# Four more Strassen steps, gate corners in another tile, a later product and quartered first weights in a hybrid pooling and convolution block (one core)

## Chip, cores and metric

The kernel runs on one core of a Trainium2 chip. The metric is the device time of one execution in microseconds (us); of the kernel before, three runs gave a median of 2419.91 us.

## What is computed

One decoder block on 256 tokens of width 4096, in float32: a norm, one large projection, two mixers, a gated merge, a projection back with a residual, and a norm.

```python
h = rmsnorm(x, norm_w)
u_p, z_p, u_c, b_c, c_c, z_c, g_logit = split(h @ w_in)        # 4096 -> 6 x 2048 and 2 x 4096
y_pool = pool(u_p, pool_w, pool_scale) * silu(z_p)             # trailing means over 2, 4, 8, 16 tokens, less the token; a 512 x 512 map per group
y_conv = b_c * conv3(c_c * u_c, conv_w, conv_b) * silu(z_c)    # causal, depthwise, three taps
br = stack(y_pool, y_conv) @ w_branch                          # two of 2048 -> 4096
merged = sum over the two of sigmoid(g_logit + gate_b) * br
out = rmsnorm(x + merged @ w_out, final_norm_w)
```

## The kernel before, in words

**Units and steps.** All large products have one form: 256 tokens by K channels times K by 1024 columns. A *unit* is one such product for 1024 output columns. The order of the units is: for each half of the conv channels cz, cb, cu, cc (z, b, u and c of the reference), for each half of the pool channels pz and pu, then eight gate units g0_0, g1_0, g0_1 ... g1_3, eight branch units b0_0, b1_0 ... b1_3, and four output units o0 to o3. A *step* of a unit takes 256 channels of K: 16 steps in a unit, 8 in a branch unit. Its weights, 256 x 1024 floats (1 MB), come in one DMA into one of three buffers of the tile `raw`.

**Float32 in two halves.** Each operand is split into a rounded high half (an ACT copy, `highs`, L54) and a low half, the rest (a VectorE subtraction, `lows`, L57); a product is three matmuls, high x high, high x low and low x high. The halves of the weights stand in the tile `ring`, which has 15 cells of 512 columns; a cell is free again after the last matmul that reads it. The halves of the other operand (x for the first units, then the branch outputs y, then the merged m) stand in `arena`, `extra` and `last_pair`; PE loads them as stationary.

**Plain and Strassen steps.** A plain step (P) has 8 blocks of 3 matmuls. A Strassen step (S) takes the 2 x 2 blocks of its operands and needs 7 products, 21 matmuls, in Winograd's form; for that VectorE makes four sums of weight blocks (tile `parts`, 4 instructions) and takes the low halves of 3 blocks and 4 sums: `added` and `split` in `Step.rest`. An S step uses 7 ring cells, a P step 4. Which steps are S is written out by hand in strings, one character a step: FIRST, SIX4, SEVEN3, EIGHT, HOST, SIX5, OUT3, B0, B1 (L34 to L43). HOST has 19 characters: besides the 16 steps it holds B, the pooling's band product (`band_sums`, L568), and two M, its 512 x 512 maps (`mix`, L594), of the pooling unit before. It is used by pz1, which holds pu0's, and by g0_0, which holds pu1's. After the second M four groups of transposes of Y follow in ticks, and fill E.

**Banks and corners.** The sums of a unit stand in eight PSUM banks. Four (`sums`) are copied by ACT to E or Y at the unit's end (`evacuate`). If it has S steps, the other four (`shared`), the corners, are copied by ACT to a place called the join's slot, summed by VectorE there (`corner_sums`: two adds and a subtraction), and added to the unit's result (`combine`). For most units the slot is the next of the three raw buffers, so that it stands in the rotation of the weight loads as one load would (`loaded`, `issue_load`). For branch units (`rotates` False) it is `last_pair`.

**Order of work.** Every engine keeps the order in which the program was written. `pump` (L897) issues, after each block of matmuls, whatever may go: the next weight load when the step three loads back is prepared, and the next piece of preparation (highs, sums, lows) of the steps up to four ahead, if ring cells are free. After each 6 matmuls a `tick` takes one entry of a queue of small works; each unit puts its epilogue there (`epi`), in which `gap(n)` leaves n ticks free. So the small works, the roundings of later weights and the copies out of PSUM stand on ACT and VectorE in one fixed order. Ticks also run *fills* (`Fill`): an operand of the branch or output units is brought from DRAM by a DMA of the POOL queue into `sa` or `sb`, and split into halves in a freed part of `arena` by ACT or VectorE. The POOL queue also carries the gate's bias, which is added in memory by an accumulating DMA (`gather`, 512 KB each), and the moves of gates and products.

**Branch units.** b0_c's epilogue, which runs within b1_c, multiplies by the gate: `mul(Y, E, Y)`, the *product*, one tick after the unit's end. b1_c's epilogue loads the second gate, multiplies, adds Y, and transposes the sum.

**The start.** Steps 0 to 15 of the first unit, cz0, also bring x: `fetch_x` loads a block into Y, and ACT and VectorE make the operand of it, directly for a P operand, or with sums (`x_sums`) for an S operand, though cz0 itself has P steps only. Its first step's weights come in four DMAs and are rounded by quarters; the other steps are rounded by one instruction per tile. The third step uses an operand with sums.

Of the kernel before, what the change touches and what calls it, by code (L numbers as in the profile page):

```python
# [17 lines left out]
D = 4096  # L18
# [16 lines left out]
FIRST = (0, 1, 8, 2, 9, 3, 10, 11, 4, 12, 13, 5, 14, 6, 15, 7)  # L35
OPENED = 12
SIX4 = "PPPPSPSPSPSPSPSP"
SEVEN3 = "PPPSPSPSPSPSPSPS"
EIGHT = "PSPSPSPSPSPSPSPS"
HOST = "PPPBPPMMPPSPSSPSSPS"  # L40
OUT3 = "PSPSPSPSPSPSSPPP"
B0 = "PPPPPSPS"
B1 = "PSPSPSPP"  # L43


# [1 line left out]
def hybrid_block(ctx: ExitStack, tc: tile.TileContext, x, xc, prm, rows_in, w_in, pool_w, w_branch, w_out, out):  # L47
# [174 lines left out]
    class Step:  # L222
# [7 lines left out]
        def first(self):  # L230
            if self.kind == "B":
                return []

            def rounded(cells):
                self.q = self.raw.rearrange("p (i c) -> p i c", i=4)
                self.cells = cells
                if self is steps[0]:
                    for i in range(4):
                        highs(cells[i:i + 1], self.q[:, i:i + 1])
                else:  # L240
                    highs(cells, self.q[:, 0:len(cells)])

            return [(3 if self.kind == "S" else 4, None, rounded)]

        def rest(self):
            if self.kind == "P":
                def rests(_):
                    if self is steps[0]:
                        for i in range(4):
                            lows(self.cells[i:i + 1], self.q[:, i:i + 1])  # L250
                    else:
                        lows(self.cells, self.q)

                return [(None, None, rests)] + self.mid
            if self.kind == "S":
                def added(_):
                    q = self.q
                    add(sums[:, 0:2], q[:, 3:4].to_broadcast([P, 2, NH]), q[:, 1:3])
                    add(sums[:, 2], sums[:, 0], q[:, 2])
                    add(sums[:, 3], sums[:, 2], q[:, 0])  # L260
                    lows(self.cells, q[:, 0:3])

                def split(cells):
                    self.sum_cells = cells
                    highs(cells[0:2], sums[:, 0:2])
                    highs(cells[2:4], sums[:, 2:4])
                    lows(cells, sums)

                return [(None, None, added)] + self.mid + [(4, None, split)]
            if self.kind == "B":  # L270
                def parts(cells):
                    self.cells = cells
                    highs(cells, quarters(E))
                    lows(cells, quarters(E))

                return [(4, lambda: self.unit.flags.get("base"), parts)]

            def pooled(cells):
                self.pool_cells = cells
                q = quarters(E)[:, 2 * self.g:2 * self.g + 2]  # L280
                highs(cells, q)
                lows(cells, q)

            return [(None, None, lambda _: lows(self.cells, self.q)),
                    (2, lambda: self.unit.flags.get(f"pooled{self.g}"), pooled)]
# [188 lines left out]
    def in_unit(name, col, epi, text, **kw):  # L474
        units.append(Unit(name, lambda i: w_in[col // NU, i], seq_x(text), x_ops, epi, scaled=True, **kw))
        units[-1].text = text
        return units[-1]
# [4 lines left out]
    def conv_units(c, first):  # L482
        base = 2 * HALF + c * NU

        def b_epi(u):
            def copy(j):
                act(chan(Y)[:, 2 * j:2 * j + 2], bankview(j))
            return gap(6) + transposes(E, copy) + [lambda: move(g_d[c], Y)]

        def c_epi(u):  # L490
            def copy(j):
                if j == 3:
                    for i in range(4):
                        act(chan(E)[:, 2 * i:2 * i + 2], bankview(i))

            def taps(j):
                v, y = chan(E)[:, 2 * j:2 * j + 2], chan(Y)
                for i in range(2):
                    b = 2 * j + i
                    kb = 8 * c + b  # L500
                    act(y[:, b], v[:, i], AF.Identity, scale=tap_col(2, kb), bias=bias_col(kb))
                for i in range(2):
                    b = 2 * j + i
                    kb = 8 * c + b
                    for s in (1, 2):
                        stt(y[:, b, s:], v[:, i, 0:T - s], tap_col(2 - s, kb), y[:, b, s:], ALU.mult, ALU.add)

            items = gap(6) + pairs(transposes(E, copy)) + gap(1)
            for j, n in enumerate((1, 5, 7, 7)):
                items += gap(n) + [lambda j=j: taps(j)]  # L510
            return items + [lambda: move(E, g_d[c])] + gap(6) + [lambda: mul(Y, Y, E), lambda: put(y_d[1, c], chan(Y))]

        in_unit(f"cz{c}", base + 3 * HALF, lambda u: silu_y(), FIRST if first else SIX4, dst=Y)
        in_unit(f"cb{c}", base + HALF, b_epi, EIGHT).urgent = lambda: mul(E, E, Y)
        in_unit(f"cu{c}", base, lambda u: gap(2) + band_items(0) if c == 0 else [], SEVEN3, dst=Y)
        in_unit(f"cc{c}", base + 2 * HALF, c_epi, EIGHT).urgent = lambda: mul(E, E, Y)

    def pool_units(c):
# [98 lines left out]
    def gate_unit(n, c):  # L617
        def epi(u):
            def bias(t):
                gather(E[:, t], gate_b[n, None, c * NU:(c + 1) * NU].to_broadcast([P, NU]))  # L620

            return gap(1) + [lambda: bias(0), lambda: bias(1)] + gap(12) + [
                lambda: act(E[:, 0], E[:, 0], AF.Sigmoid), None,
                lambda: act(E[:, 1], E[:, 1], AF.Sigmoid), lambda: move(gates_d[n, c], E)] + (
                    [lambda: move(Y, gates_d[0, 0])] if (n, c) == (1, 3) else [])
        text = HOST if (n, c) == (0, 0) else SIX4 if (n, c) == (1, 3) else EIGHT
        in_unit(f"g{n}_{c}", 6 * HALF + n * D + c * NU, epi, text)

    def spare():
        return last_pair["tile"].rearrange("p (a n) -> p a n", a=2)  # L630
# [1 line left out]
    def branch_unit(n, c):  # L632
        def epi(u):
            if n == 0:
                return gap(1) + [lambda: mul(Y, E, Y)]
            turned = spare() if c < 3 else Y

            def gated():
# [245 lines left out]
    def issue_load(s):  # L884
        i = s.load_index
        r = raw[:, i % NRAW]
        if isinstance(s, Join):
            s.slot = r.rearrange("p (i c) -> p i c", i=4)
            return
        if i == 0:  # L890
            for k in range(4):
                load(r[:, k * NH:(k + 1) * NH], s.src[:, k * NH:(k + 1) * NH])
        else:
            load(r, s.src)
        if i + 1 < 16:
            fetch_x(i + 1)
        s.raw = r  # L897
# [60 lines left out]
            state["limit"] = state["now"] + u.lead  # L958
        pump()

    fetch_x(0)
    pump()

    def room(o):
# [36 lines left out]
    for u in units:  # L1001
# [1 line left out]
            last_pair["stack"].close()  # L1003
            open_last(F32)
        if not u.rotates:
            u.join.slot = last_pair["tile"].rearrange("p (i c) -> p i c", i=4)
        if u is last_x:
            bands_open.close()
            more = ctx.enter_context(tc.tile_pool(name="more", bufs=1))
# [121 lines left out]
```

## Time and profile before

| | |
|---|---|
| median of 3 runs | 2419.91 us (2418.51 to 2421.69) |
| the profiled execution | 2420.03 us |
| its span, first to last instruction | 2418.3 us |
| matmuls on PE | 10515 |
| ACT busy | 1421.8 us (59%) |
| bytes moved | 547.07 MB, 226 GB/s |
| mean granted clock of PE | 0.994 |

The span is what the trace covers; 1.7 us of the time lie around it. PE is TensorE's matmuls, PEld its weight loads, DVE is VectorE, ACT ScalarE, POOL and SP the two that issue DMAs. L57 and L54 are helpers that issue nearly all VectorE and ACT work, so the tiles of a row say what it is: `ring<-raw` on ACT is a rounding of weights, on VectorE a low half; `parts` are Strassen sums, `raw<-raw` and `last_pair<-last_pair` on VectorE are corner sums, `E<-sums` on ACT is a copy out of PSUM. A row of the timeline tells start, duration, engine, line, operation, tiles, shape and count, and in brackets how long the engine was idle before it and what ended that.

### The profile page before, as it was taken

How to read it: one execution, taken by the hardware profiler on the slowest of the kernel's cores; microseconds unless marked ns; L12 is line 12 of the kernel's file. 1: busy time of each engine (PE TensorE's matmuls, PEld its weight loads, DVE VectorE, ACT ScalarE, POOL GpSimd, SP SyncE). 2: the span in 40 equal slices, each digit the busy share in tenths (PEclk: the TensorE clock that was granted, in tenths of full speed). 3: DMA queues.
4: the chain of work that ended last, by engine and by line, in shares of the span. 5: the costliest groups of instructions: out<-in, count | busy, mean ns of one | idle time of the engine just before them, and what ended most of it. 6: DMA issues, size and time to landing. Idle time of an engine off the chain costs nothing. (4 is left out here: it accounts for less than half of the span.)

```text
span 2418.3 us, 26848 instructions
## 1 busy us (share of the span) xinstructions
PE 2379.8 (98%) x10515; PEld 1960.6 (81%) x10515; DVE 2137.6 (88%) x1769; ACT 1421.8 (59%) x1367; POOL 85.6 (4%) x147
## 2 busy tenths in 40 slices
PE   8999999999999999999999999999899999999998
PEld 6888888888888888888888888888778887888886
DVE  8789989988989969969998999889788889899998
ACT  6655555655556556556666566665565555556664
POOL 0000000000000000000000000001100000000000
PEclk9999999999999999999999999999999999999999
DMA  8656546655646655655776576667666765758767
GB/s 331 225 193 226 191 175 244 234 199 204 220 177 231 228 192 192 225 191 187 266 244 204 215 261 242 209 224 272 229 245 212 264 233 208 257 192 273 246 217 267
DMA packets 82959, 547.07 MB, mean 226 GB/s; under 512 B 9488, under 2 KB 9488, under 8 KB 21776
## 3 DMA queue, kind: packets, MB, share of 16 engines
q1 hardware_dynamic: 69392, 485.52, 55.1%
q0 software_dynamic: 13008, 58.73, 8.0%
q8 instruction: 82, 1.34, 0.2%
q10 hardware_dynamic: 432, 1.11, 0.1%
q14 instruction: 45, 0.37, 0.0%
HBM read 519.10 MB, written 26.21 MB: 225 GB/s over the span
## 5 line engine op out<-in xcount | busy, mean ns | idle before, releaser
L937 PE MATMUL sums<-ring,arena 128*128 128x512 f32 x7515 | 1756.9, 391 | 20.5 <-DVE ring L57 9.4
L937 PEld LDWEIGHTS sums<-ring,arena 128*128 128x128 f32 x7515 | 1412.2, 188 | 319.7 <-DVE ring L57 12.3
L57 DVE TENSOR_TENSOR ring<-raw,ring 128x2048 fp32r<-128x2048 f32 (+3 forms) x526 | 938.6, 1796 | 167.0 <-ACT ring L54 163.5
L54 ACT ACTIVATE ring<-raw 128x2048 fp32r<-128x2048 f32 (+3 forms) x526 | 791.4, 1520 | 493.9 <-PE sums L937 270.9
L54 ACT ACTIVATE ring<-parts 128x1024 fp32r<-128x1024 f32 (+1 forms) x403 | 400.2, 1007 | 384.2 <-DVE parts L57 341.6
L937 PE MATMUL shared<-ring,arena 128*128 128x512 f32 x2100 | 509.2, 391 | 1.5 <-DVE ring L57 1.5
L57 DVE TENSOR_TENSOR ring<-parts,ring 128x2048 fp32r<-128x2048 f32 (+3 forms) x225 | 434.9, 1946 | 44.5 <-ACT ring L54 43.6
L937 PEld LDWEIGHTS shared<-ring,arena 128*128 128x128 f32 x2100 | 396.3, 189 | 86.3 <-DVE ring L57 3.6
L57 DVE TENSOR_TENSOR parts<-parts,raw 128x512 f32<-128x512 f32 x378 | 262.0, 693 | 12.9
L57 DVE TENSOR_TENSOR parts<-raw 128x1024 f32<-128x1024 f32 x189 | 230.8, 1221 | 7.5 <-DMA raw<-in_w_in_dram 7.2
L937 PE MATMUL sums<-ring,last_pair 128*128 128x512 f32 x366 | 89.8, 396 | 0.0
L937 PEld LDWEIGHTS sums<-ring,last_pair 128*128 128x128 f32 x366 | 68.9, 188 | 16.5
L57 DVE TENSOR_TENSOR raw<-raw 128x512 f32<-128x512 f32 (+1 forms) x66 | 57.3, 868 | 10.9 <-ACT raw L54 9.3
L54 ACT ACTIVATE E<-sums,rin 128x512 f32<-128x512 f32 x56 | 36.0, 687 | 25.5 <-PE sums L937 25.4
L54 ACT ACTIVATE raw<-shared 128x512 f32<-128x512 f32 x88 | 47.0, 606 | 0.3
L937 PE MATMUL shared<-ring,last_pair 128*128 128x512 f32 x168 | 41.6, 396 | 0.0
L937 PEld LDWEIGHTS shared<-ring,last_pair 128*128 128x128 f32 x168 | 31.6, 188 | 7.7
L69 DVE SCALAR_TENSOR_TENSOR E<-raw,rin,E 128x1024 f32<-128x1024 f32 x28 | 34.7, 1280 | 0.2
L54 ACT ACTIVATE last_pair<-shared 128x512 f32<-128x512 f32 x44 | 24.2, 600 | 13.8 <-PE shared L422 13.1
L57 DVE TENSOR_TENSOR E<-E,last_pair 128x2048 f32<-128x2048 f32 x12 | 27.4, 2287 | 2.2 <-ACT E L54 2.2
L78 POOL DMA_DIRECT2D E<-in_rows_dram x16 | 13.9, 867 | 434.4 <-DVE E L69 432.3
L54 ACT ACTIVATE E<-sums 128x512 f32<-128x512 f32 x44 | 25.6, 596 | 2.9 <-PE sums L937 0.5
(118 smaller groups left out, 553.9 us busy)
## 6 DMA issues: line engine op xcount, KB each, us to landing
raw<-in_w_in_dram SPq DMA_DIRECT2D x319, 1024.0 KB, 4.8
raw<-in_w_branch_dram SPq DMA_DIRECT2D x64, 1024.0 KB, 4.8
raw<-in_w_out_dram SPq DMA_DIRECT2D x64, 1024.0 KB, 4.8
E<-in_rows_dram POOLq DMA_DIRECT2D x16, 512.0 KB, 11.2
gates_d<-E POOLq DMA_DIRECT2D x8, 1024.0 KB, 8.2
Y<-in_xc_dram SPq DMA_DIRECT2D x16, 256.0 KB, 6.4
raw<-in_pool_w_dram SPq DMA_DIRECT2D x4, 1024.0 KB, 7.2
Y<-gates_d POOLq DMA_DIRECT2D x4, 1024.0 KB, 6.1
```

Of the source, the lines that this page charges most:

```text
L54: return pin(nc.scalar.activation(dst, src, func, **kw))
L57: return pin(nc.vector.tensor_tensor(out=dst, in0=a, in1=b, op=op))
L69: return pin(nc.vector.scalar_tensor_tensor(out=dst, in0=a, scalar=s, in1=b, op0=op0, op1=op1, **kw))
L78: return pin(nc.gpsimd.dma_start(dst, src, accum_op=ALU.add))
L937: pin(nc.tensor.matmul(ps, lhs, rhs, start=n == 0, stop=n == u.total[b] - 1))
```

## The change

- SEVEN3, for the u units cu0 and cu1, becomes EIGHT3: 8 S steps in place of 7. HOST, for pz1 and g0_0, gets 7 S steps in place of 6; one P step less stands between the second M and the first S, and the string ends in SS. That is one S more in each of four units.
- The corners of the gate units go to Y, and these units no longer take a raw buffer in the rotation. (Of the units with HOST that is g0_0; pz1 keeps a raw buffer.)
- The product of b0_c runs 8 ticks after the unit's end plus one, in place of 1 plus one.
- B0 has its two S steps as the fifth and seventh of eight, in place of the sixth and eighth.
- The weights of the second step of cz0 come in four DMAs too, and are rounded and subtracted by quarters; the first block of x is loaded behind the first quarter of the first weights, in place of ahead of it.

```diff
-SEVEN3 = "PPPSPSPSPSPSPSPS"
+EIGHT3 = "PPPSSPSPSPSSPSPS"
-HOST = "PPPBPPMMPPSPSSPSSPS"
+HOST = "PPPBPPMMPSPSSPSSPSS"
-B0 = "PPPPPSPS"
+B0 = "PPPPSPSP"
...
-                if self is steps[0]:
+                if self in steps[:2]:
                     for i in range(4):
                         highs(cells[i:i + 1], self.q[:, i:i + 1])
...
-                    if self is steps[0]:
+                    if self in steps[:2]:
                         for i in range(4):
                             lows(self.cells[i:i + 1], self.q[:, i:i + 1])
...
-        in_unit(f"cu{c}", base, lambda u: gap(2) + band_items(0) if c == 0 else [], SEVEN3, dst=Y)
+        in_unit(f"cu{c}", base, lambda u: gap(2) + band_items(0) if c == 0 else [], EIGHT3, dst=Y)
...
-        in_unit(f"g{n}_{c}", 6 * HALF + n * D + c * NU, epi, text)
+        in_unit(f"g{n}_{c}", 6 * HALF + n * D + c * NU, epi, text).rotates = False
...
             if n == 0:
-                return gap(1) + [lambda: mul(Y, E, Y)]
+                return gap(8) + [lambda: mul(Y, E, Y)]
...
-        if i == 0:
+        if i < 2:
             for k in range(4):
                 load(r[:, k * NH:(k + 1) * NH], s.src[:, k * NH:(k + 1) * NH])
+                if i == k == 0:
+                    fetch_x(0)
...
-    fetch_x(0)
     pump()
...
         if not u.rotates:
-            u.join.slot = last_pair["tile"].rearrange("p (i c) -> p i c", i=4)
+            u.join.slot = quarters(Y if u.name[0] == "g" else spare())
```

## The prediction

> **What bounds the kernel now.** I read the page first, then the chain of waits, the groups of instructions by shape, busy time by stretch, and last the timelines around each idle stretch of PE.
>
> ```profile
> PE 2379.8 (98%) x10515; PEld 1960.6 (81%) x10515; DVE 2137.6 (88%) x1769; ACT 1421.8 (59%) x1367; POOL 85.6 (4%) x147
> ...
> E<-in_rows_dram POOLq DMA_DIRECT2D x16, 512.0 KB, 11.2
> ...
> raw<-in_w_branch_dram SPq DMA_DIRECT2D x64, 1024.0 KB, 4.8
> ```
>
> The chain of waits (start, duration, what):
>
> ```profile
> 2104.72 2.72 PE shared L937 x12
> ```
>
> PE is the bound: 2.72/12 = 0.227 us for a matmul. 10515 at that pace are 2384 us of the span of 2418.3, so some 35 us are stalls. What can be won is stalls, or matmuls. VectorE (DVE), 88% busy, comes next, and most late stalls are its. Its prices, by shape (busy, mean ns of one):
>
> ```profile
> L57 DVE TENSOR_TENSOR ring<-raw,ring 128x2048 fp32r<-128x2048 f32 x212 | 484.5, 2288 | 149.6 <-ACT ring L54 149.6
> L57 DVE TENSOR_TENSOR ring<-raw,ring 128x1536 fp32r<-128x1536 f32 x203 | 356.0, 1753 | 11.2 <-ACT ring L54 7.9 <-PE sums L937 3.2
> L57 DVE TENSOR_TENSOR ring<-parts,ring 128x2048 fp32r<-128x2048 f32 x153 | 350.0, 2287 | 42.0 <-ACT ring L54 41.2
> L57 DVE TENSOR_TENSOR parts<-parts,raw 128x512 f32<-128x512 f32 x378 | 262.0, 693 | 12.9
> L57 DVE TENSOR_TENSOR parts<-raw 128x1024 f32<-128x1024 f32 x189 | 230.8, 1221 | 7.5 <-DMA raw<-in_w_in_dram 7.2
> ```
>
> A plain step (P) costs VectorE 2.29 us and PE 24 matmuls, 5.44 us. A Strassen step (S) costs VectorE 1.22 + 2 x 0.69 + 1.75 + 2.29 = 6.65 us and PE 21 matmuls, 4.76 us. So each swap of P for S takes 0.68 us from PE and gives VectorE 4.36 us.
>
> **The change part by part.**
>
> **(a) Early weights by quarters.** Timeline of the start (start, duration, engine; in brackets idle time and what ended it), then busy time by stretch (PE, PEld, DVE, ACT, POOL, granted clock, DMA share, GB/s):
>
> ```profile
> 13.08 1.91 ACT L54 ACTIVATE ring<-raw 128x2048 fp32r<-128x2048 f32 x1 [1.57 <-DMA raw<-in_w_in_dram]
> 15.02 2.29 DVE L57 TENSOR_TENSOR ring<-raw,ring 128x2048 fp32r<-128x2048 f32 x1 [2.99 <-ACT ring L54]
> 15.04 0.50 PE L937 MATMUL sums<-ring,arena 128*128 128x512 f32 x1 [1.94 <-ACT ring L54]
> 16.26 1.91 ACT L54 ACTIVATE ring<-raw 128x2048 fp32r<-128x2048 f32 x1 [0.47 <-DMA raw<-in_w_in_dram]
> 17.37 8.86 PE L937 MATMUL sums<-ring,arena 128*128 128x512 f32 x27 [1.82 <-DVE ring L57]
> 20.42 2.28 DVE L57 TENSOR_TENSOR ring<-raw,ring 128x2048 fp32r<-128x2048 f32 x1
> 30.65 9.01 PE L937 MATMUL sums<-ring,arena 128*128 128x512 f32 x39
> ```
>
> ```profile
> 13.00:17.40 4.40, 0.64 (x3) 0.22 (x2) 2.38 (x2) 3.85 (x4) 0.00 (x0) 0.82 0.99 407
> 17.40:22.50 5.10, 5.10 (x12) 4.05 (x13) 4.96 (x9) 4.37 (x7) 0.00 (x0) 0.50 0.80 276
> 1715.50:1719.00 3.50, 3.42 (x8) 2.74 (x9) 3.40 (x7) 2.22 (x5) 0.00 (x0) 0.50 0.00 0
> 1776.00:1783.70 7.70, 4.90 (x15) 3.58 (x14) 7.63 (x7) 5.29 (x4) 0.00 (x0) 0.79 0.40 136
> ```
>
> The second step waits for whole-tile roundings: its first matmul for ACT's 1.91 us, its second for VectorE's 2.29 us. Then it runs 5.1 us at a clock of 0.50. By quarters each wait is about a quarter of that, and nearly ends before the first step's matmuls do (15.04 less 1.94 idle: 13.1). The next limit is the third step: its weights are rounded from 16.26 to 18.17. VectorE's work on that step's operand (17.3 to 20.4 now) comes behind the second step's low halves, so about 14.6 to 17.9, and the third step's low halves end at 18.2 + 2.29 = 20.5. 23 matmuls later, at 25.7, the third step is done; now it is at 30.65. That is -4.9. [...] I take **-4.3**, from -2.5 to -4.9.
>
> [...]
>
> **(b) Four S steps: two in the u units (cu0, cu1), two in the units with bands and mixing (pz1, g0_0).** Busy time by stretch: cu0, pz1 and, for (f), b1_3 from its first steps on.
>
> ```profile
> 183.70:267.90 84.20, 84.20 (x380) 69.57 (x379) 75.23 (x60) 49.87 (x49) 5.27 (x23) 1.00 0.58 216
> 852.70:952.10 99.40, 99.40 (x462) 82.79 (x461) 80.43 (x66) 58.55 (x59) 5.97 (x8) 1.00 0.55 201
> 2025.20:2062.70 37.50, 33.84 (x137) 27.46 (x136) 37.10 (x35) 18.67 (x19) 2.15 (x4) 0.91 0.48 165
> ```
>
> VectorE is idle 9.0 and 19.0 us in them (cu1 and g0_0 are built like them), so 4.36 more has room. PE: 4 x 3 x 0.227 = -2.7. In pz1 and g0_0 one plain step less stands between the second mixing product and the first S, and VectorE's order changes: that step's sums (4.4 us) now stand ahead of the second mixing multiply. Now:
>
> ```profile
> 889.89 4.48 DVE L57 TENSOR_TENSOR ring<-raw,ring 128x2048 fp32r<-128x2048 f32 x2
> 894.28 1.29 DVE L57 TENSOR_TENSOR Y<-shared,Y 128x512 f32<-128x512 f32 x2
> ...
> 897.48 0.60 PE L422 MATMUL shared<-ident,Y 128*128 128x128 f32 x4
> ```
>
> The multiply then ends at 889.89 + 2.29 (one of the two) + 4.4 + 1.3 = 897.9, and the transposes at 897.48 need it: 0.45 us twice, +0.9. Two S in a row at the end of these units leave VectorE about 1 us later at the unit boundary: I allow 0.7 for both. Net **-1.1**; from -2.7 (all hidden) to 4 x 3.68 = +14.7 (nothing hidden); the idle time says near the low end.
>
> **(c) Gate corners in Y: the gap in front of b0_0.** The copies and sums are the same instructions on another tile (0); what changes is the rotation of the three raw buffers, of which a gate unit's corners now take none.
>
> ```profile
> 1699.03 2.29 DVE L57 TENSOR_TENSOR ring<-raw,ring 128x2048 fp32r<-128x2048 f32 x1
> 1702.66 5.78 PE L937 MATMUL sums<-ring,last_pair 128*128 128x512 f32 x24
> 1704.02 2.29 DVE L57 TENSOR_TENSOR ring<-raw,ring 128x2048 fp32r<-128x2048 f32 x1
> 1705.05 1.08 ACT L54 ACTIVATE raw<-shared 128x512 f32<-128x512 f32 x2
> 1706.34 3.13 SPq L72 DMA_DIRECT2D raw<-in_w_branch_dram  x2
> 1713.05 1.91 ACT L54 ACTIVATE ring<-raw 128x2048 fp32r<-128x2048 f32 x1 [6.91 <-DMA raw<-in_w_branch_dram]
> 1714.86 2.41 ACT L54 ACTIVATE E<-sums,rin 128x512 f32<-128x512 f32 x4
> 1715.59 6.65 PE L937 MATMUL sums<-ring,arena 128*128 128x512 f32 x21 [7.14 <-ACT E L54]
> ```
>
> This is the longest stall. g1_3 ends at 1708.44; its four copies out of PSUM stand on ACT behind the rounding of b0_0's third weights, which waits for their DMA. That load was issued at 1706.34, when the low halves that began at 1704.02 had freed its buffer, since g1_3's corners hold one of the three. With corners in Y it takes the buffer that is free at 1699.03 + 2.29 = 1701.3; plus 4.8 us it lands at 1706.1. ACT rounds to 1708.1, then copies the sums; PE starts at about 1708.9 instead of 1715.6, -6.7, and the half clock after the gap (3.5 us at 0.50, above: half of it) goes too, 1.7: **-8.4**, from -7 to -9. In the other gate units PE doesn't stall, so nothing else is won there.
>
> **(d) b0_0 and b1_0, (e) b1_1 and b1_2, (f) b1_3 and the start of o0: product later, S one step earlier in the b0 units.**
>
> ```profile
> 1772.62 2.29 DVE L57 TENSOR_TENSOR Y<-E,Y 128x2048 f32<-128x2048 f32 x1
> ...
> 1779.22 1.44 PE L937 MATMUL sums<-ring,arena 128*128 128x512 f32 x5 [2.80 <-DVE ring L57]
> ...
> 1867.18 1.43 PE L937 MATMUL sums<-ring,arena 128*128 128x512 f32 x5 [0.58 <-DVE ring L57]
> ...
> 2025.22 2.29 DVE L57 TENSOR_TENSOR ring<-parts,ring 128x2048 fp32r<-128x2048 f32 x1 [2.43 <-ACT ring L54]
> ...
> 2044.22 2.50 PE L937 MATMUL sums<-ring,arena 128*128 128x512 f32 x5 [3.65 <-DVE ring L57]
> ```
>
> Each b1 unit stalls in its second S, whose sums stand behind the boundary's work and the product (2.29 us). Seven ticks later the product stands behind that S.
>
> (d) In b1_0 2.80 us of idle go, 1.6 of lost clock (7.70 us at a mean of 0.79): -4.4. But the stage now runs 8 us earlier, and one fill of a stationary operand comes by a transfer behind the bias gathers (11.2 us above):
>
> ```profile
> sa<-y_d POOLq DMA_DIRECT2D x1, 256.0 KB, 12.9
> ```
>
> ACT's copy for that fill stands ahead of the roundings for b0_0's sixth and seventh steps. The gathers start when VectorE has added g1_3's corners: from 1709.1 (end of the second weights' low halves) it has four pieces of work of 2.3 to 2.7 us by the prices above (corner sums, low halves, an operand's sums, the adding), so about 1719; the fill then lands around 1734 to 1736, and the sixth step, due at 1735.5, could wait 0 to 4 us for its low halves. I take +1.9, near the middle: **-2.5**, from -4.4 to +1.6 (4 us of wait and a new half clock).
>
> (e) 0.58 us of idle each: **-1.2**, from -1.2 to 0.
>
> (f) Here VectorE is busy 37.10 of 37.50 us, so moving the product only moves the wait to the next S: won is what VectorE idles, the 2.43 us at 2025.22 (the corner sums of b0_3 now come a step earlier), and part of the half clock. **-3.0**, from 0 to -5.5.
>
> **Sum.** -4.3 - 1.1 - 8.4 - 2.5 - 1.2 - 3.0 = -20.5. The profiled execution took 2420.03 us, 1.7 around its span and 0.1 off the median of 2419.91: **2399.5 us**.
>
> **The rivals.**
>
> A. VectorE has more room than I count: the fill is early, b1_3's wait goes whole, the S steps are free. a -4.9, b -2.7, c -9.0, d -4.4, e -1.2, f -5.5: -27.7, **2392.3**. For it: cu0 and pz1 leave 9.0 and 19.0 us of VectorE idle, and the fill's 12.9 us were taken beside three weight loads. Against: 37.10 of 37.50 in (f).
>
> B. The fill behind the gathers is late: (d) is +1.6 and (f) is 0, the others stand: -13.4, **2406.6**. For it the 12.9 us; against it, fewer weight loads compete with the gathers once (c) has sent them earlier.
>
> [...]
>
> D. The other side: VectorE's queue is the path wherever S steps follow each other. Then each new S hands PE 3.68 us, and with a wait above 2.8 us a half clock too (0.50 for 3.5 us, 1.7 lost): 4 x 5.4 = +21.5, and (d), (e), (f) give nothing, since VectorE sets them. -4.3 - 8.4 + 21.5: **2428.8**. It decides where VectorE's idle time in a unit is below 4.36; the rows have 9.0 and 19.0.
>
> E. The change doesn't do what it says: the third weights of b0_0 stay late, the quarters land no sooner than the whole did, the S steps cost what they save, and the later product only moves its wait, as in (f). Every term is 0: **2420.0**.
>
> **How the numbers follow.** Forecast 0.51, A 0.18, B 0.15, C 0.08, D 0.05, E 0.03. By the bounds the forecast's own range is 2393 to 2404; with A and B, and the unknown ends of (b) and (f), 2390 to 2408 leaves out D, E and a tail of each. 0.2% (4.8 us) is about what a measurement of this kernel can tell from no change: faster 0.92, same 0.03, slower 0.05.
>
> **What would show it.** PE has 12 matmuls less (10503). (a) No clock of 0.50 near 17 to 22 us, and the third step done by 26. (c) No ACT wait of 6.9 us on in_w_branch in front of b0_0, PE's gap there below 1 us. (d) The longest PE wait in b0_0 and b1_0 below 3 us; if above, ACT's operand copy waits for a y_d transfer. (f) A wait of 2 to 4 us left in b1_3, now at its third S. (b) In pz1, g0_0 and the units behind them waits of 1 us or less; several above 2 us mean D. The prediction is wrong if the b units together hold as much PE idle time as now.

## The result, and the profile after

The changed kernel takes 2396.49 us (median of 4, 2394.66 to 2398.32) against 2419.42 us of the kernel before (4 runs, 2418.51 to 2421.69): a ratio of 0.9904, 95% interval 0.9887 to 0.9921. The forecast was 2399.5 us. The profiled execution took 2398.32 us, with a span of 2396.5.

The sum came near. Several of its terms did not: some gave more than forecast, one gave half, and one gave nothing. The page's first row shows the 12 matmuls that went:

```profile
PE 2370.2 (99%) x10503; PEld 1954.5 (82%) x10503; DVE 2153.1 (90%) x1803; ACT 1428.0 (60%) x1390; POOL 86.6 (4%) x147
```

10503 at 2.72/12 us are 2381 us of the span, which leaves 16 us for stalls, start and end, where 35 were left before.

**By stage.** If the matmuls of the program are counted in order in the trace, the start of each unit can be read off. The table tells the starts of five units and the change between them. The forecast of each stage is the sum of the prediction's terms that lie in it; term (c) lies in two stages, its gap (6.7) and its half clock (1.7; *half clock* is time in which the granted clock is 0.50 and the matmuls start 0.43 us apart in place of 0.23, so that about half of it is lost). One profile a kernel stands behind each measured figure; how far they scatter is seen in the table of the experiments.

| stage | before, from to | after, from to | forecast | measured |
|---|---|---|---|---|
| start to cb0: (a) | 0 to 101.92 | 0 to 96.17 | -4.3 | -5.75 |
| cb0 to g1_3: (b) | to 1624.50 | to 1618.16 | -1.1 | -0.59 |
| g1_3 to b0_0: gap of (c) | to 1715.59 | to 1701.33 | -6.7 | -7.92 |
| b0_0 to b1_3: half clock of (c), (d), (e) | to 2024.54 | to 2001.57 | -5.4 | -8.71 |
| b1_3 to o2: (f) | to 2242.44 | to 2220.90 | -3.0 | +1.43 |
| o2 to the end | to 2418.3 | to 2396.5 | 0 | -0.26 |

**The start.** Timeline of after, then its busy time in the same stretches as in the prediction, with cu0, pz1 and b1_3 behind them:

```profile
6.87 16.10 PE L939 MATMUL sums<-ring,arena 128*128 128x512 f32 x63 [1.76 <-ACT ring L54]
...
14.58 1.92 ACT L54 ACTIVATE ring<-raw 128x2048 fp32r<-128x2048 f32 x1 [1.58 <-DMA raw<-in_w_in_dram]
...
16.53 2.29 DVE L57 TENSOR_TENSOR ring<-raw,ring 128x2048 fp32r<-128x2048 f32 x1 [0.22 <-ACT ring L54]
...
24.91 6.29 PE L939 MATMUL sums<-ring,arena 128*128 128x512 f32 x27
```

```profile
13.00:17.40 4.40, 4.40 (x22) 3.62 (x21) 4.01 (x9) 2.72 (x3) 0.00 (x0) 1.00 1.03 421
17.40:22.50 5.10, 5.10 (x24) 4.24 (x23) 5.07 (x8) 4.33 (x5) 0.00 (x0) 1.00 1.02 387
177.90:261.40 83.50, 83.50 (x377) 68.98 (x376) 79.17 (x62) 50.95 (x51) 7.26 (x23) 1.00 0.61 216
847.30:946.30 99.00, 99.00 (x459) 82.21 (x459) 83.14 (x71) 59.67 (x62) 4.93 (x8) 1.00 0.56 202
2002.20:2039.70 37.50, 34.22 (x144) 27.54 (x144) 36.67 (x36) 18.44 (x19) 2.34 (x5) 0.95 0.54 185
```

From 6.87 us PE waits for nothing through the first steps; where it ran at a clock of 0.50 before (17.40 to 22.50), it now runs at 1.00. The third step ended at 30.65 before, and now ends at 24.91. VectorE's idle time in cu0 fell from 9.0 to 4.3 us, and PE stayed busy throughout. In b1_3 VectorE is nearly as full as before, 36.67 of 37.50 us.

**In front of b0_0.** Timeline of after:

```profile
1693.44 8.13 SPq L72 DMA_DIRECT2D raw<-in_w_branch_dram  x3
...
1700.38 2.41 ACT L54 ACTIVATE E<-sums,rin 128x512 f32<-128x512 f32 x4
...
1701.33 23.31 PE L939 MATMUL sums<-ring,arena 128*128 128x512 f32 x102
...
1710.28 0.88 POOL L78 DMA_DIRECT2D E<-in_rows_dram  x1 [0.66 <-DVE E L69]
...
1724.40 0.63 ACT L54 ACTIVATE arena<-sa 128x512 fp32r<-128x512 f32 x1 [6.67 <-DMA sa<-y_d]
```

The third weights of b0_0 are now fetched at 1693.44, and ACT copies the sums at 1700.38 with no wait for weights ahead of it; PE goes on without any gap, where it idled 7.14 us. The gathers start at 1710.28, and the fill behind them is there at 1724.40. PE waits 0.2 us for it at the sixth step.

**b1_3 and the start of o0.** Timeline of after:

```profile
2022.07 2.28 DVE L57 TENSOR_TENSOR Y<-E,Y 128x2048 f32<-128x2048 f32 x1
...
2031.38 2.50 PE L939 MATMUL sums<-ring,arena 128*128 128x512 f32 x5 [3.14 <-DVE ring L57]
...
2068.50 2.28 DVE L57 TENSOR_TENSOR E<-E,Y 128x2048 f32<-128x2048 f32 x1
...
2070.84 1.10 PE L422 MATMUL shared<-ident,E 128*128 128x128 f32 x8 [2.02 <-DVE E L57]
```

Here is the loss that is left: PE idles 3.14 us at b1_3's third S step, as forecast, and then 2.02 us in o0 for a sum that its transposes need, which wasn't. The wait at those transposes in before:

```profile
2094.51 1.09 PE L422 MATMUL shared<-ident,E 128*128 128x128 f32 x8 [1.22 <-DVE E L57]
```

### The profile page after: what moved, and what is told of

It is laid out like the page before. It is cut to its first block, busy times and chain, and to the rows that moved or that the text cites. A ratio compares the mean times of both kernels' runs of the same rounds, so it can differ in the third digit from the quotient of the medians.

```text
span 2396.5 us, 26919 instructions
## 1 busy us (share of the span) xinstructions
PE 2370.2 (99%) x10503; PEld 1954.5 (82%) x10503; DVE 2153.1 (90%) x1803; ACT 1428.0 (60%) x1390; POOL 86.6 (4%) x147
## 5 line engine op out<-in xcount | busy, mean ns | idle before, releaser
L57 DVE TENSOR_TENSOR ring<-raw,ring 128x1536 fp32r<-128x1536 f32 (+3 forms) x538 | 936.7, 1755 | 134.8 <-ACT ring L54 134.2
L54 ACT ACTIVATE ring<-raw 128x1536 fp32r<-128x1536 f32 (+3 forms) x538 | 789.7, 1487 | 411.2 <-PE sums L939 245.3
L54 ACT ACTIVATE ring<-parts 128x1024 fp32r<-128x1024 f32 (+1 forms) x414 | 409.6, 1002 | 429.6 <-DVE parts L57 392.4
L57 DVE TENSOR_TENSOR ring<-parts,ring 128x2048 fp32r<-128x2048 f32 (+3 forms) x235 | 444.8, 1907 | 35.6 <-ACT ring L54 35.1
L939 PE MATMUL sums<-ring,last_pair 128*128 128x512 f32 x336 | 82.8, 396 | 0.0
L57 DVE TENSOR_TENSOR raw<-raw 128x512 f32<-128x512 f32 (+1 forms) x42 | 36.5, 868 | 9.3 <-ACT raw L54 8.4
L54 ACT ACTIVATE raw<-shared 128x512 f32<-128x512 f32 x56 | 29.7, 610 | 0.5 <-DVE ring L57 0.2
L54 ACT ACTIVATE Y<-shared 128x512 f32<-128x512 f32 x44 | 23.8, 598 | 6.3 <-PE shared L422 6.2
```

The lines of the kernel that those rows point to most:

```text
L54: return pin(nc.scalar.activation(dst, src, func, **kw))
L57: return pin(nc.vector.tensor_tensor(out=dst, in0=a, in1=b, op=op))
L939: pin(nc.tensor.matmul(ps, lhs, rhs, start=n == 0, stop=n == u.total[b] - 1))
```

## The experiments

My theory was the prediction's: the quartered rounding won the start, the buffer rotation the gap, and the place of the product the waits in the b1 units; in b1_3 VectorE sets the pace. The time is the median of four runs, the stages are those of one profile; a unit that an edit doesn't touch shows how far one profile scatters from the next. "Loss" in the texts is what the spacings of a unit's matmuls exceed 0.227 us by, added up (excesses of 0.06 us and more). The ratio is to the kernel before, run on the same chip.

| kernel | time, us | ratio, 95% | to cb0 | cb0 to g1_3 | g1_3 to b0_0 | b0_0 to b1_3 | b1_3 to o2 |
|---|---|---|---|---|---|---|---|
| before | 2419.42 | 1 | 101.92 | 1522.59 | 91.08 | 308.95 | 217.90 |
| changed | 2396.49 | 0.9904 (0.9887 to 0.9921) | 96.17 | 1521.99 | 83.17 | 300.24 | 219.33 |
| w_whole | 2396.34 | 0.9909 (0.9894 to 0.9924) | 97.53 | 1521.41 | 83.17 | 298.56 | 217.83 |
| x_first | 2396.80 | 0.9911 (0.9896 to 0.9926) | 98.28 | 1521.05 | 83.17 | 298.96 | 219.37 |
| rotate | 2405.85 | 0.9950 (0.9935 to 0.9965) | 96.87 | 1520.91 | 92.37 | 300.76 | 219.03 |
| gap1 | 2397.61 | 0.9915 (0.9898 to 0.9931) | 97.18 | 1521.09 | 83.17 | 298.57 | 219.57 |
| old_s | 2396.18 | 0.9906 (0.9892 to 0.9921) | 97.10 | 1522.44 | 83.89 | 298.69 | 216.30 |
| old_b0 | 2402.68 | 0.9932 (0.9917 to 0.9947) | 96.73 | 1522.13 | 85.11 | 302.81 | 218.87 |
| old_b0_gap1 | 2406.22 | 0.9944 (0.9927 to 0.9960) | 97.43 | 1521.47 | 85.30 | 307.58 | 218.65 |
| pool_product | 2398.73 | 0.9918 (0.9903 to 0.9933) | 97.20 | 1521.25 | 83.17 | 299.17 | 219.54 |
| b13_order2 | 2394.68 | 0.9899 (0.9884 to 0.9914) | 96.22 | 1521.14 | 83.52 | 299.12 | 217.70 |
| late_turn | 2395.01 | 0.9901 (0.9884 to 0.9918) | 96.26 | 1520.71 | 83.36 | 299.68 | 216.66 |
| act_cast | 2408.72 | 0.9957 (0.9942 to 0.9972) | 96.86 | 1522.09 | 86.08 | 305.07 | 220.61 |
| both_late | 2392.49 | 0.9889 (0.9873 to 0.9906) | 96.63 | 1520.63 | 83.18 | 300.06 | 214.36 |

Apart from w_whole and x_first all changed kernels have the same start, and reach cb0 at 96.2 to 97.4 us, on average 96.8. In these eleven PE waits for nothing between its first matmuls and cb0. What sets cb0's start is when the half clock of the start ends, read from the spacing of the matmuls alone (0.43 us, then 0.23; the clock column of the profile shows 1.00 there): at 10.0 us in the earliest and 12.7 in the latest, and each microsecond of it costs about half of one.

### w_whole: one load for the second step's weights, rounded by quarters

```diff
-        if i < 2:
+        if i < 1:
             for k in range(4):
                 load(r[:, k * NH:(k + 1) * NH], s.src[:, k * NH:(k + 1) * NH])
```

> The changed kernel, with the second step's weights fetched by one load again; they are still rounded and subtracted by quarters, and x still comes behind the first quarter. Theory 1 (what cost time was the rounding of a whole tile, 1.91 us on ACT and then 2.29 us on VectorE, with PE waiting for each): the 1 MB lands by about 11.4 us, the first quarter is rounded 0.6 us later and its low half ready at about 12.7, and PE is at work on the first step until about 14: no wait, start and time as the changed kernel's within 0.5 us (about 2396.5). Rival (the gain came from splitting the transfer, so that rounding can begin before the whole has landed, or from the quarters of the first weights no longer sharing the DMA engines with a large load: the fourth of them landed at 9.77 us before and at 7.58 after): PE waits 1 to 4 us in the first two steps and the time is 2398 to 2401.

Timeline of its start:

```profile
6.95 17.39 PE L939 MATMUL sums<-ring,arena 128*128 128x512 f32 x63 [1.83 <-ACT ring L54]
...
11.56 2.19 ACT L54 ACTIVATE ring<-raw 128x512 fp32r<-128x512 f32 x4 [1.59 <-DMA raw<-in_w_in_dram]
12.23 2.50 DVE L57 TENSOR_TENSOR ring<-raw,ring 128x512 fp32r<-128x512 f32 x4 [1.74 <-ACT ring L54]
```

The weights land at 11.5 and the quarters are rounded from 11.56 on; PE, at work since 6.95, waits for none of them. The time is the changed kernel's. cb0 starts at 97.53, 0.1 us behind the latest of the others; the half clock of the start ends later here too, at 13.0, which accounts for it. So splitting the transfer brings nothing that can be seen, and the theory stands.

### x_first: x ahead of the first weights again

```diff
-                if i == k == 0:
-                    fetch_x(0)
...
+    fetch_x(0)
     pump()
```

> The changed kernel, with the first block of x loaded ahead of the first weights again. Theory 1 (the place of x does not matter for the end, the third step's weights do): PE starts at about 5.95 us instead of 6.87, and as the third step's low halves are ready only 0.5 us before PE needs them, between 0 and 0.9 us are won: 2395.6 to 2396.5. Rival (the move of x is what brought the start its gain beyond the 4.3 us forecast, since it let the first weights land earlier): the fourth quarter of the first weights lands near 9.8 us again, and the first unit ends 1.4 us or more later than in the changed kernel: 2397.9 or more.

Timeline of its start:

```profile
5.53 12.64 PE L937 MATMUL sums<-ring,arena 128*128 128x512 f32 x49 [0.41 <-ACT ring L54]
...
17.64 2.29 DVE L57 TENSOR_TENSOR ring<-raw,ring 128x2048 fp32r<-128x2048 f32 x1 [0.22 <-ACT ring L54]
...
19.99 5.07 PE L937 MATMUL sums<-ring,arena 128*128 128x512 f32 x14 [1.82 <-DVE ring L57]
```

PE starts at 5.53, 1.3 us earlier than in the changed kernel, but VectorE reaches the third step's low halves at 17.64 instead of 16.53, and PE waits 1.82 us for them and runs at half clock again (a mean of 0.55 from 20.00 to 23.00). cb0 starts at 98.28, 1.5 us behind the average of the others: the rival's size, though in one profile, and the time itself differs by less than it scatters (by the time alone neither range is met). That the transfers are later is seen in busy time by stretch, of x_first and then of w_whole (where x is second):

```profile
5.00:8.00 3.00, 2.59 (x10) 2.03 (x9) 2.13 (x5) 1.74 (x3) 0.00 (x0) 1.00 0.86 238
```

```profile
5.00:8.00 3.00, 1.17 (x4) 0.86 (x4) 1.95 (x4) 2.47 (x5) 0.00 (x0) 1.00 0.99 345
```

238 GB/s moved in place of 345. What holds the transfers back with x in front wasn't tried.

### rotate: the gate units' corners in a raw buffer

```diff
-        in_unit(f"g{n}_{c}", 6 * HALF + n * D + c * NU, epi, text).rotates = False
+        in_unit(f"g{n}_{c}", 6 * HALF + n * D + c * NU, epi, text)
```

> The changed kernel, with the gate units' corners in a raw buffer of the rotation again (in place of Y). Theory 1 (the corners hold the buffer for which the third weights of b0_0 wait): that load is issued some 5 us later, PE idles about 7 us in front of b0_0 and runs 3.5 us at half clock, so the time is 7 to 9 us longer, 2403.5 to 2405.5, and no gate unit before it changes. b0_0 and b1_0 then lose no more than their 1.6 us of the changed kernel, as the fill behind the gathers has more time. Rival (the gap went because the four S steps and the other edits moved VectorE's work in front of it): the time stays within 2 us of 2396.5.

Timeline in front of b0_0:

```profile
1701.45 17.62 SPq L72 DMA_DIRECT2D raw<-in_w_branch_dram  x5
...
1707.52 2.00 ACT L54 ACTIVATE ring<-raw 128x1536 fp32r<-128x1536 f32 x2 [6.19 <-DMA raw<-in_w_branch_dram]
...
1709.43 2.40 ACT L54 ACTIVATE E<-sums,rin 128x512 f32<-128x512 f32 x4
1710.15 19.15 PE L939 MATMUL sums<-ring,arena 128*128 128x512 f32 x74 [6.51 <-ACT E L54]
```

The third weights are fetched at 1701.45 (1693.44 in the changed kernel), ACT waits 6.19 us for them with the copies of the sums behind it, and PE idles 6.51. The stage is 9.2 us longer and the time 9.4: the theory, but 0.4 us beyond its upper end. b0_0 loses 8.8 us, of them 6.7 at the gap, and g1_3 loses 2.4 us at two of its S steps, where the theory had no gate unit change.

### gap1: the product early again

```diff
-                return gap(8) + [lambda: mul(Y, E, Y)]
+                return gap(1) + [lambda: mul(Y, E, Y)]
```

> The changed kernel, with the product one tick after the unit's end plus one again, in place of eight. Theory 1 (the product stands ahead of the sums of the second S step in each b1 unit; in b1_3 and o0, where VectorE is busy all the time, its place only moves the wait): b1_0 loses 3 to 5.5 us more, b1_1 and b1_2 1 us each, b1_3 and o0 together stay at their 10.1 us within 1.5: 2401.5 to 2404. Rival (in b1_3 the later product is what pushes the transposes of o0's start behind VectorE's work, 2.2 us and a half clock): b1_3 and o0 together lose 2 to 4 us less than in the changed kernel, and the time is 2398 to 2400.5. Second rival (S one step earlier in the b0 units, and not the place of the product, won the waits in the b1 units): 2396 to 2398.

Timeline of b1_0, which starts at 1743.62 here:

```profile
1751.38 2.29 DVE L57 TENSOR_TENSOR Y<-E,Y 128x2048 f32<-128x2048 f32 x1
1753.14 7.64 PE L939 MATMUL sums<-ring,arena 128*128 128x512 f32 x33
1753.58 1.22 DVE L57 TENSOR_TENSOR parts<-raw 128x1024 f32<-128x1024 f32 x1
```

The product stands ahead of the second S step's sums, as before, and no b1 unit up to b1_2 loses anything. Theory 1, which is the prediction's, fell here; so did the first rival: o0 loses 5.6 us, not less than the changed kernel's 5.0. The second rival remains: the order of the b0 units.

### old_b0 and old_b0_gap1: S as sixth and eighth, with the late and with the early product

```diff
-B0 = "PPPPSPSP"
+B0 = "PPPPPSPS"
```

> The changed kernel, with the S steps of the b0 units as sixth and eighth again; the product stays at its later place. Theory 1 (either edit alone removes the wait in front of the second S step of the b1 units: an earlier S in b0 leaves VectorE less to do at the boundary, a later product leaves it less to do after the boundary): b1_0, b1_1 and b1_2 lose under 1.2 us together, time 2395.5 to 2398.5. Rival (the order of the b0 units alone removes it): they lose 5 to 7.5 us together, as before, time 2401 to 2404. In b1_3 and the start of o0 both expect the loss of all kernels so far, 9 to 10.5 us.

> The changed kernel, with both edits of the branch units taken back: S as sixth and eighth in b0, product one tick after the unit's end plus one. Theory 1 (these two edits are what removed the waits of b1_0, b1_1 and b1_2): they come back, 2.8 us of idle and 1.6 to 2.7 of half clock in b1_0, 1.0 in each of the others and 0.8 in b0_3: 5.5 to 8 us more, 2402 to 2404.5. Rival (the gap in front of b0_0 had put the whole stage out of step, and the corners in Y alone removed the waits): under 2 us more, 2396.5 to 2398.5.

Timeline of b1_0 in old_b0_gap1, where it starts at 1747.20, and then in old_b0:

```profile
1759.86 2.29 DVE L57 TENSOR_TENSOR Y<-E,Y 128x2048 f32<-128x2048 f32 x1
...
1766.32 2.28 DVE L57 TENSOR_TENSOR ring<-parts,ring 128x2048 fp32r<-128x2048 f32 x1
...
1766.46 1.93 PE L939 MATMUL sums<-ring,arena 128*128 128x512 f32 x5 [2.80 <-DVE ring L57]
```

```profile
1764.05 1.43 PE L939 MATMUL sums<-ring,arena 128*128 128x512 f32 x5 [0.47 <-DVE ring L57]
```

With both edits undone the 2.80 us of before are back to the digit, and the stage b0_0 to b1_3 takes 307.58 us. The late product alone brings it to 302.81, the new order alone (gap1) to 298.57, and both to 300.24 in the changed kernel and 298.6 to 300.1 in the others that share its stage and have no gap in front of it. So the order does the whole work (9.0 us), and the product adds nothing to it; without the new order the late product would have won about half of that (4.8). A reason can be read in the rows: in gap1 VectorE takes the product 7.76 us after the unit's start, in old_b0_gap1 12.66 us after: with an S less to prepare at the boundary VectorE is 4.9 us further ahead, and 2.29 us of product no longer matter. The time of old_b0_gap1, 2406.22, is 1.7 us beyond theory 1: g1_3 loses 1.5 us there and b0_0 another 0.7, which the theory had not named. For old_b0 neither expectation held whole (the time, 2402.68, is in the rival's range): b1_0 loses 2.7 us, b1_1 and b1_2 nothing, and a part of its 6 us comes from places neither had named: 1.3 in g1_3, 0.8 in b0_3 (transposes), and 0.7 as a wait in front of b0_0.

### old_s: the four new S steps taken back

```diff
-EIGHT3 = "PPPSSPSPSPSSPSPS"
-HOST = "PPPBPPMMPSPSSPSSPSS"
+EIGHT3 = "PPPSPSPSPSPSPSPS"
+HOST = "PPPBPPMMPPSPSSPSSPS"
```

> The changed kernel, with the four new S steps taken back (the strings SEVEN3 and HOST of before). Theory 1 (VectorE's idle time pays for the S steps, but its later finish shows behind cu0 and cu1, in cz1, cb1, pz0 and pu0, which lost 2.9 us before and lose 4.0 to 5.0 in the changed kernel): PE has 12 matmuls more, 2.7 us, and these four units lose 1.1 to 2.1 us less; the time is 0.6 to 1.6 us longer, about 2397.6. Rival (the waits in those four units are a matter of phase and not of the S steps): they stay at 4 to 5 us and the time is 2.7 us longer, 2399.2. Rival on the other side (each S step costs PE more than it saves): 2395 or less.

The stage cb0 to g1_3, where the four S steps are, takes 1522.44 us (1522.59 before), against 1521.32 on average over the twelve profiles that have them (1520.63 to 1522.13): by this one profile they win 1.1 us, against a scatter of 1.5 among the twelve. PE's saving is 2.7; the rest is lost in cz1, cb1, pz0 and pu0, which lose 2.7 us here, 2.9 before and 3.7 to 5.3 with the S steps. The longest of these waits, in the changed kernel at cb1's first matmul:

```profile
430.72 0.50 PE L939 MATMUL sums<-ring,arena 128*128 128x512 f32 x1 [1.05 <-ACT Y L54]
```

By stages theory 1 holds. The time doesn't show it: 2396.18, no longer than with the S steps. The profile has less loss in o0 (3.0 us), a place that the edit doesn't reach and that scatters from 3.0 to 5.0 us over the kernels with the same code in the branch and output units. So the S steps' gain rests on the stage alone; that they don't cost 3.68 us each, as in rival D, is plain.

### pool_product: the last product on GpSimd

```diff
-                return gap(8) + [lambda: mul(Y, E, Y)]
+                return gap(8) + [lambda: pin(nc.gpsimd.tensor_tensor(out=Y, in0=E, in1=Y, op=ALU.mult)) if c == 3 else mul(Y, E, Y)]
```

> The changed kernel, with the last product (that of b0_3, within b1_3) computed by GpSimd in place of VectorE. Theory 1 (VectorE has more work in b1_3 than PE, so only work taken from it shortens the wait at the third S step): the wait there, 3.3 us in the changed kernel, falls by 2.3 us to about 1.0, and with it the half clock behind it (1.4 us); b1_3 and o0 together lose 2 to 4.5 us less than their 10.1, time 2392 to 2394.5. Rival (the product on GpSimd takes so much longer, or slows VectorE so much while it runs, that the sum in b1's epilogue waits for it): same time or up to 6 us longer. Rival (the wait is for the weights or for ACT, not for VectorE): the wait at the third S stays above 2.5 us.

Timeline of b1_3:

```profile
2013.50 4.73 POOL L635 TENSOR_TENSOR Y<-E,Y 128x2048 f32<-128x2048 f32 x1
2013.82 5.69 DVE L57 TENSOR_TENSOR parts<-parts,raw 128x512 f32<-128x512 f32 x2
...
2021.23 2.50 PE L939 MATMUL sums<-ring,arena 128*128 128x512 f32 x5 [4.41 <-DVE ring L57]
```

GpSimd takes 4.73 us for the 2.29 us of VectorE, and beside it two additions of VectorE that take 1.42 us elsewhere (the prediction counted 0.69 for one) take 5.69. The wait at the third S is gone, but PE now idles 4.41 us at the second, and b1_3 loses 7.0 us instead of 5.1. That is the first rival. It agrees with VectorE as the limit, but doesn't settle it.

### b13_order2 and late_turn: two ways to give VectorE time

```diff
-        text = B1 if n else B0
+        text = ("PSPSPPSP" if c == 3 else B1) if n else B0
```

> The changed kernel, with the third S step of b1_3 alone one step later (PSPSPPSP in place of PSPSPSPP). Theory 1 (VectorE has more work in the whole stretch from b0_3's end to o0's transposes than PE, so the wait only moves): the 3.3 us of wait at the third S shrink, but what is won there comes back in o0, whose transposes wait for the sum that VectorE now reaches later; b1_3, o0 and o1 together lose 9 to 11.5 us as in the other kernels, time 2395 to 2398.5. Rival (the wait is one of order: a plain step of 5.4 us on PE and 2.3 on VectorE ahead of the third S gives VectorE 3.1 us, and the rest of the stretch has room): the wait falls under 0.7 us, the half clock behind it goes, o0 stays as it is, time 2391.5 to 2393.5.

Timeline of b1_3 and o0 (the row at 2028.37 is the plain step that now comes ahead of the third S):

```profile
2028.37 6.88 PE L939 MATMUL sums<-ring,arena 128*128 128x512 f32 x29 [1.69 <-DVE ring L57]
...
2067.62 1.24 PE L422 MATMUL shared<-ident,E 128*128 128x128 f32 x8 [2.36 <-DVE E L57]
```

The wait in b1_3 falls to 1.69 and moves to the plain step; the one in o0 rises from 2.02 to 2.36. b1_3, o0 and o1 lose 9.0 us, 10.7 in the changed kernel: the low end of theory 1, with the time 0.3 us below its range. Part of the wait is order, part is too much work.

The second way leaves VectorE's order alone:

```diff
-                lambda: c < 3 and move(Y, gates_d[0, c + 1])] + gap(3) + pairs(transposes(E, copy)) + [stored]
+                lambda: c < 3 and move(Y, gates_d[0, c + 1])] + gap(3 if c < 3 else 7) + pairs(transposes(E, copy)) + [stored]
```

> The changed kernel, with the four groups of transposes in b1_3's epilogue (they run within o0) four ticks later; VectorE's order is not changed by that. Theory 1 (the wait of 2.2 us in o0 is only that PE's transposes are written too early in its order, VectorE is late for them and for nothing else; 3.4 us after them VectorE idles 5 us): the wait goes, and the half clock behind it, o0 loses 2 to 3.6 us less, time 2393 to 2394.5. Rival (VectorE is late for the weights too): PE waits instead for the low halves or sums of o0's next steps, o0 loses as much as now, 4 to 5.6 us, time 2395.5 to 2398.5.

Timeline of o0:

```profile
2066.91 2.29 DVE L57 TENSOR_TENSOR E<-E,Y 128x2048 f32<-128x2048 f32 x1
...
2072.83 1.03 PE L422 MATMUL shared<-ident,E 128*128 128x128 f32 x8
```

The transposes wait no more, and the next steps' weights are not late in their place: o0 loses 2.0 us instead of 5.0, most of it in two waits of 0.6 and 0.7 near its end. Theory 1: this wait was one of PE's order alone. The time, 2395.01, is 0.5 us above its range.

### act_cast: a rounding from VectorE to ACT

```diff
                 if self.phase == 1:
-                    copy(o.view[:, 0], q)
+                    act(o.view[:, 0], q)
```

> The changed kernel, with the rounding of a stationary operand that has sums (0.63 us, in a fill) done by ACT in place of VectorE. Two of them stand in VectorE's queue ahead of the third S of b1_3, two more ahead of o0's transposes. Theory 1 (VectorE's work is what these two waits last): each gets 1.2 us shorter, so 3.3 becomes about 2.0 and 2.2 about 1.0, and one or both half clocks go (1.0 to 1.4 us each); b1_3, o0 and o1 lose 2.4 to 4.8 us less, time 2391.7 to 2394. Rival (ACT's roundings stand behind the extra work and become late, or VectorE has to wait for ACT between the sums and the low half): nothing won, 2395.5 to 2399.

Timeline in front of b0_0:

```profile
1704.27 1.28 ACT L54 ACTIVATE E<-sums,rin 128x512 f32<-128x512 f32 x2
1705.02 2.92 PE L939 MATMUL sums<-ring,arena 128*128 128x512 f32 x6 [2.74 <-ACT E L54]
...
1709.68 0.95 ACT L54 ACTIVATE arena<-sb 128x896 fp32r<-128x896 f32 x1 [4.13 <-DVE sb L57]
1710.54 1.25 ACT L54 ACTIVATE E<-sums,rin 128x512 f32<-128x512 f32 x2
...
1711.26 2.08 PE L939 MATMUL sums<-ring,arena 128*128 128x512 f32 x4 [3.31 <-ACT E L54]
```

The worst of the runs, 12 us slower than the changed kernel, and not by what either theory named: the moved rounding needs VectorE's sums, so ACT stands 4.13 us for VectorE, and behind it stand two of the copies that free the banks for PE, which idles 3.31 us. A like wait of ACT, 4.68 us at 1695.48, stands ahead of PE's first gap of 2.74 us. b0_0 loses 9.4 us. The third S of b1_3 waits as before (3.26 us), so nothing was won there either.

### both_late: the two edits that won something, together

> The changed kernel with both of the last edits that won something: the third S step of b1_3 one step later, and the transposes of b1_3's epilogue four ticks later. Theory 1 (VectorE is late in b1_3 by 2 to 3 us of work, which PE must wait out once, and the wait at the transposes is one of order alone): b1_3 keeps about 2.4 us of loss, the start of o0 loses under 0.5 us, o0 and o1 together 2 to 3 us; b1_3, o0 and o1 lose 4.4 to 5.5 us against 10 in the changed kernel, time 2390.5 to 2393. Rival (what is taken from the one wait falls to the next: with the earlier waits gone VectorE is late for o0's first S): b1_3, o0 and o1 lose 7 to 9 us, time 2393.5 to 2396.

Timeline of b1_3 and o0:

```profile
2028.86 3.48 PE L939 MATMUL sums<-ring,arena 128*128 128x512 f32 x14 [1.71 <-DVE ring L57]
...
2071.07 1.03 PE L422 MATMUL shared<-ident,E 128*128 128x128 f32 x8
```

2392.49 us (2391.92 to 2394.05): 4.0 us less than the changed kernel's median, with all four times below that kernel's four. b1_3 keeps 2.4 us of loss as expected; o0 and o1 lose 3.7, more than expected, in four waits of 0.5 to 0.8 us, three of them late in o0 and in o1, where they had been one of 1.3 and one of 0.3. Their sum, 6.1 us, lies between the two theories, the time within the first.

## Why the prediction was right

The total was right by 3 us, and in part by luck: by stages (d) and (e) won 3.3 us more than forecast, the start 1.5 and the gap 1.2, while (f) fell 4.4 short and (b) 0.5. Point by point:

- **(a)** Right in kind, 0.2 to 1.5 us too small. The reasoning about roundings holds: PE no longer waits for them. "The next limit is the third step" does not. Its low halves were ready at 18.8 (16.53 and 2.29) instead of the forecast 20.5, and in none of the eleven profiles did PE wait for them; what is left of the limit is the half clock of the start. That the third step then ends at 24.9 to 26.2, around the forecast 25.7, is luck. The later x, of which no gain was forecast, let the weights land earlier: ACT has the third step's at 14.58 us, and at 15.69 with x in front (x_first); there the low halves are ready at 19.9, PE waits for them, and the start takes 1.5 us longer, of the 5.1 won on average. The forecast took 0.6 us off the 4.9 that it had worked out, and 2.4 at the low end of its range, for the later x and for four loads in place of one. That was the author's estimate, and no run shows such a cost: with x in front cb0 starts later, at 98.28, and with one load (w_whole, a DMA share of 0.99 in the row from 5.00 to 8.00 above) the time is 2396.34 us, the changed kernel's. The gain came from the split rounding and, by x_first, from the order of the loads.
- **(b)** Near in size: 1.1 forecast, 0.6 between the two profiles and 1.1 by old_s, both within the scatter of 1.5. That the sizes agree is luck, since the places were wrong. The forecast put 0.9 us at the transposes of pz1 and g0_0, where nothing of that size shows, and 0.7 at the unit ends; what is lost, 0.8 to 2.5 us, is in the units two and three behind cu0 and cu1. That VectorE's idle time is what pays stands as argued: in cu0 half of it went, with no stall.
- **(c)** Right, at the upper end: 7.3 us of gap and 1.7 of half clock went, 9.0 in all, and rotate brought back 8.8 in b0_0.
- **(d) and (e)** Forecast 3.7, measured 7.0 (the stage's 8.71 less 1.7). Two steps failed. "The fill, +1.9": its bounds were right, its middle was not; the fill landed with 0.2 us to wait or none. (The upper bound of (d) also adds up to 1.3, not 1.6: 4 us of wait and 1.7 of half clock less 4.4.) And "each b1 unit stalls in its second S, whose sums stand behind the boundary's work and the product", from which I took the product's place as the cause: gap1 shows that it is worth nothing beside the earlier S of the b0 units, which also freed b0_3 (0.8) and which I had only counted in (f).
- **(f)** Wrong: 3.0 forecast, 1.4 lost. "A wait of 2 to 4 us left in b1_3" held (3.14). What failed is "won is what VectorE idles": VectorE is busy there nearly without a pause, and the next place where PE needs it, o0's transposes, wasn't in the sum. PE loses 1.5 us less in b1_3, but VectorE starts the sum for the transposes only 0.7 us earlier (66.9 us after b1_3's start, 67.6 before). So a wait of 1.4 us (beyond the spacing) became one of 2.2, with 1.2 us of half clock behind it. Over the five profiles with the same code in the branch and output units the stage takes 216.3 to 219.4 us (217.90 before): 219.0 to 219.4 in the three with a half clock behind this wait, less in the two without. So what this profile lost is in part chance, but in none of the five were 3.0 us won. late_turn shows that this second wait was avoidable, by PE's order.
- **Rival A** was right on (a), (c), (d) and (e), wrong on (b) and (f). **B** fell with the fill, which was not late. **D** (each S step handing PE 3.68 us) is excluded by old_s; **E** by rotate and old_b0_gap1.

What stays open: why cz1 and pz0, two units behind a unit with a new S step, wait; why x in front slows the first transfers; why b1_0's first matmul still waits, 0.9 us in the changed kernel; and how much of b1_3's remaining 1.7 us is VectorE's work and how much order.

## What to carry to other kernels

Where an engine is full over a stretch, a wait removed at one place must be looked for at every later instruction that needs that engine, up to its first idle time; only there is it known whether anything was won. When two edits remove the same wait, test each without the other: here one did everything, and the other, which alone would have won half, added nothing. And before work is moved to an engine that is half idle, look at what stands behind it in that engine's queue: two such moves made the kernel slower, by 2 and 12 us, though GpSimd was 4% and ACT 60% busy.

## What the hardware showed beyond that

- **VectorE was slower beside GpSimd.** In pool_product two VectorE additions took 5.69 us beside one GpSimd multiplication of 4.73 us, 4.3 us longer than the 1.42 that they take elsewhere. What held them back was not shown.
- **The half clock comes after waits shorter than I took.** After the first 30 us, over all fourteen profiles, none of 31 waits of 1.0 to 2.0 us (beyond the spacing of 0.227) brought a half clock, one of two at 2.1 did, and 22 of 23 from 2.15 up had one (one of these fell into a half clock already running); the prediction had put the point at 2.8. Of these waits the profile before has 2.96, 3.81 and 7.31 us with a half clock, the profile after 2.18 and 3.30; their longest without one is 1.38 us.
- **The first half clock is not fixed either.** In the eleven profiles with the same code at the start it ended, by the spacing of the matmuls, between 10.0 and 12.7 us. 2.7 us of half clock are 1.3 us of time, and about as much is the scatter of cb0's start (96.2 to 97.4); the two go together from profile to profile.
